# Decoder trunk: the opening reordered, small transfers postponed, modulation sums in every second projection step, their vectors to columns through DRAM

## The chip, the cores and the metric

The kernel runs on one core of one Trainium2 chip, in one launch. The metric is device time in microseconds (us); beside it a profile of one execution is read. TensorE (PE) multiplies matrices, VectorE (DVE), ScalarE (ACT) and GpSimd (POOL) work element by element, and SyncE (SP) issues most of the transfers (DMAs). Each engine runs its own list of instructions strictly in order, and waits on semaphores for the other engines and for DMAs.

## The reference, cut to what matters

Two layers, 512 rows of 1024 float32 each. A conditioning vector c gives six vectors of 1024 per layer (`mod`): shift, scale and gate for each half of the layer.

```python
cond = jax.nn.silu(c)
for l in range(DEPTH):                                   # 2
    mod = cond @ w_mod[l] + b_mod[l]                     # w_mod[l]: 1024 x 6144
    sh1, sc1, ga1, sh2, sc2, ga2 = [m[:, None, :] for m in jnp.split(mod, N_MOD, axis=-1)]

    h = rms_norm(x, g_norm1[l]) * (1.0 + sc1) + sh1
    z = h @ w_in[l]                                      # 1024 x 2560
    qa, ka, va, ub, qc, kc, vc = jnp.split(z, cuts, axis=-1)
    ...                                                  # heads, rms norm with gains, rope; three mixers ya, yb, yc
    y = jnp.concatenate([ya, yb, yc], axis=-1) @ w_out[l]
    x = x + ga1 * y

    h = rms_norm(x, g_norm2[l]) * (1.0 + sc2) + sh2
    x = x + ga2 * hier_moe(h, ...)                       # 32 experts, top 2 of one group
return x
```

## The kernel before

A layer is `front(l)` and then the experts (`moe`). The **opening** of `front` computes the first two of the six vectors (number i=0: shift and scale of the first half), normalizes x (`norm1`, ACT and DVE), transposes it on PE (L407), and splits each of its eight column blocks into a high and a low part (ACT L310, DVE or POOL L311), because a product of float32 is made of three passes (`mm3`, L314 to L316).

Then come the **projections**: five chunks of eight steps, step number 8c+j. A step is 12 matmuls of 128x512. Two steps share one megabyte of `w_in`, halves of which are split by ACT (L310) and POOL (L311) a little ahead (`split_next`). At a chunk's end the results go from PSUM to SBUF (`copy`, L320 on DVE and L322 on ACT, in turn). While chunk c runs, DVE, ACT and POOL normalize and rotate the heads of chunk c-1 (`rope_work`, L485 to L496, with tables that `tables` makes on POOL, L383 and L386), and PE transposes them (`heads_T`, L501). During the fifth chunk (UV) and after it run the mixers, PE's output projection, and the router.

**The modulation.** A product of the vector c with 1024 x 2048 of `w_mod` is read as eight pieces of 1 MB. For i=0 PE multiplies (`mod_unit`, L245). For i=1 (gate of the first half, shift of the second) and i=2 (scale and gate of the second) DVE adds up the pieces (`mod_part`, L253 and L255, 128x2048 each), one a step from step g on, PE adds over the partitions at step e (`mod_sum`, L260), and DVE adds the bias (`mod_row`, L270): the vectors then lie along one partition. `PLAN[l]` is (g, e) of i=1 and (g, e) of i=2. At step e + `LATER[l]` `mod_finish` brings a vector into columns, one number a partition, by 16 small matmuls with an identity (`to_cols`, L281) and a small DVE operation (L292, L297, L299), and spreads a gate over 128 partitions by way of DRAM (L288 writes `ga_d`, L289 reads it). The i=0 product of layer 1 is made by PE among the mixers of layer 0 (`one_mod`).

**Order.** PE, ACT, DVE and POOL are ordered by a scheduler; the PE and POOL work is also moved across the source's order. SP's queue is in the order of the program: all weights go through an arena of 1 MB buffers in the fixed order of `stream` (a planner sorts by the step at which each is needed, `want_layer`), and `pump` issues the next one as soon as a buffer is free. A DMA that has to wait on SP holds all that are behind it. The DMAs of SP and ACT use eight semaphores (DMAHW0 to 7) in turn, those of POOL eight others (DMASW); an instruction that uses one again waits for the DMA that had it before.

## Time and profile before

| | |
|---|---|
| median of 3 runs | 1226.66 us (1225.65 to 1226.69) |
| profiled execution, device time | 1228.5 us |
| its span | 1225.7 us |
| PE busy | 1072.6 us (88%) |
| DVE busy | 654.8 us (53%) |
| ACT busy | 358.2 us (29%) |
| POOL busy | 326.1 us (27%) |
| DMA, mean | 269 GB/s |

The span is that of the profiled execution from its first to its last instruction; the device time has 2.8 us more around it. Busy shares are means over stages with different limits: layer 0's front lies at about 0 to 285 us of the span, its experts from there to about 620, layer 1's front at about 620 to 880 and its experts behind. Views of stretches of the span tell more than the totals.

### The profile page before, as it was taken

The page shows a single profiled execution, that of the slowest core. Times are in us where ns is not written, and L with a number is a line of the kernel's source. Part 1 is how long each engine was busy: PE and PEld are TensorE (multiplying, and loading weights), DVE is VectorE, ACT ScalarE, POOL GpSimd, SP SyncE. Part 2 cuts the span into 40 slices and gives each one's busy share as a digit, 9 for nine tenths or more (in the row PEclk, how much of TensorE's full clock was granted, in tenths as well). Part 3 has the DMA queues.
Part 4 walks back from the last instruction along what each step waited for, and adds up shares of the span by engine and source line. Part 5 has one row for each costly group of instructions (what it writes and reads, how often), then busy time and mean ns, then how long its engine had stood idle before and what let it go on. Part 6 is the DMA issues. An engine that isn't in the chain of part 4 may idle for free. (4 is left out here: it accounts for less than half of the span.)

```text
span 1225.7 us, 14999 instructions
## 1 busy us (share of the span) xinstructions
PE 1072.6 (88%) x5134; PEld 627.1 (51%) x5134; DVE 654.8 (53%) x1333; ACT 358.2 (29%) x906; POOL 326.1 (27%) x259
## 2 busy tenths in 40 slices
PE   3878879999999988998877789999999999899784
PEld 2656757567783333333326567676778333333232
DVE  2779965657752222222269999767786222122127
ACT  2223223546441211111104233446643111111110
POOL 2585542000121211121116454520022312022010
PEclk9888988979989999999988898999999999999997
DMA  9946424752675999999995625352168899999993
GB/s 332 398 151 241 172 69 125 241 210 69 244 272 173 409 408 399 405 376 388 402 362 226 240 94 198 121 177 70 37 242 305 294 406 409 406 396 390 386 401 128
DMA packets 90476, 330.13 MB, mean 269 GB/s; under 512 B 18421, under 2 KB 22709, under 8 KB 75729
## 3 DMA queue, kind: packets, MB, share of 16 engines
q1 hardware_dynamic: 74248, 308.07, 66.0%
q0 software_dynamic: 15056, 18.01, 4.9%
q10 hardware_dynamic: 1016, 2.18, 0.5%
q8 instruction: 73, 1.20, 0.4%
q14 instruction: 83, 0.67, 0.2%
HBM read 339.10 MB, written 30.95 MB: 302 GB/s over the span
## 5 line engine op out<-in xcount | busy, mean ns | idle before, releaser
L1091 PE MATMUL ps<-unit,unit 128*64 128x512 f32 x1120 | 269.5, 607 | 19.1 <-DMA unit<-w 18.8
L314 PE MATMUL ps<-unit,unit 128*128 128x512 f32 x448 | 190.7, 432 | 16.4 <-DVE unit L320 16.0
L315 PE MATMUL ps<-unit,unit 128*128 128x512 f32 x448 | 185.3, 414 | 9.6 <-POOL unit L311 8.4
L1091 PEld LDWEIGHTS ps<-unit,unit 128*64 128x64 f32 x1120 | 88.7, 140 | 188.3 <-issue 171.6
L316 PE MATMUL ps<-unit,unit 128*128 128x512 f32 x448 | 183.0, 412 | 0.5 <-DVE unit L311 0.5
L1111 PE MATMUL ps<-unit,unit 128*64 128x512 f32 x560 | 140.0, 622 | 16.2 <-PEq L1159 14.5
L1096 DVE SCALAR_TENSOR_TENSOR unit<-ps,slot_f,unit 128x256 f32<-128x256 f32 x35 | 16.9, 484 | 248.7 <-ACT unit L1095 248.7
L311 POOL TENSOR_TENSOR unit<-unit,unit 128x1024 fp32r<-128x1024 f32 (+1 forms) x46 | 120.8, 2631 | 79.6 <-ACT unit L310 79.6
L1060 POOL DMA_INDIRECT unit<-xn_d,slot_i x62 | 63.1, 1018 | 288.6 <-PE ps L1071 158.0
L1095 ACT ACTIVATE unit<-ps 128x256 f32<-128x256 f32 x35 | 13.5, 385 | 392.5 <-PE ps L1091 392.5
L310 ACT ACTIVATE unit<-unit 128x1024 fp32r<-128x1024 f32 (+1 forms) x92 | 88.2, 964 | 133.1 <-PE ps L316 71.0
L314 PEld LDWEIGHTS ps<-unit,unit 128*128 128x128 f32 x448 | 90.2, 202 | 44.2 <-DVE unit L320 18.1
L315 PEld LDWEIGHTS ps<-unit,unit 128*128 128x128 f32 x448 | 90.4, 202 | 30.0 <-POOL unit L311 9.6
L316 PEld LDWEIGHTS ps<-unit,unit 128*128 128x128 f32 x448 | 89.4, 200 | 21.3 <-DVE unit L311 1.2
L1125 DVE TENSOR_TENSOR unit<-ps,unit 128x512 f32<-128x512 f32 x62 | 42.9, 692 | 84.6 <-PE ps L1111 84.6
L255 DVE SCALAR_TENSOR_TENSOR unit<-unit,csil,unit 128x2048 f32<-128x2048 f32 x28 | 85.0, 3034 | 0.4
L1111 PEld LDWEIGHTS ps<-unit,unit 128*64 128x64 f32 x560 | 36.1, 139 | 92.5 <-issue 60.5
L512 ACT ACTIVATE unit<-unit,sm 128x512 f32<-128x512 f32 (+3 forms) x96 | 53.3, 556 | 37.8 <-DVE sm L510 37.3
L1080 DVE TENSOR_SCALAR unit<-ps,cols 128x128 f32<-128x128 f32 x132 | 45.1, 404 | 33.5 <-PE ps L1071 33.5
L311 DVE TENSOR_TENSOR unit<-unit,unit 128x1024 fp32r<-128x1024 f32 (+1 forms) x46 | 56.6, 1236 | 9.4 <-ACT unit L310 8.7
L1065 POOL DMA_INDIRECT y_d<-unit,slot_y x31 | 31.5, 1016 | 111.3 <-DVEq L1161 46.5
L322 ACT ACTIVATE unit<-ps 128x512 f32<-128x512 f32 (+3 forms) x82 | 39.4, 487 | 73.1 <-PE ps L316 31.7
(215 smaller groups left out, 1409.7 us busy)
## 6 DMA issues: line engine op xcount, KB each, us to landing
unit<-w SPq DMA_DIRECT2D x256, 512.0 KB, 13.4
unit<-w SPq DMA_DIRECT2D x64, 1024.0 KB, 14.9
unit<-w_mod SPq DMA_DIRECT2D x48, 1024.0 KB, 4.7
unit<-w_in SPq DMA_DIRECT2D x16, 1024.0 KB, 14.2
y_d<-k_zero SPq DMA_DIRECT2D x16, 512.0 KB, 10.7
unit<-w_out SPq DMA_DIRECT2D x8, 1024.0 KB, 7.1
unit<-y_d SPq DMA_DIRECT2D x16, 512.0 KB, 12.0
unit<-w_in SPq DMA_DIRECT2D x8, 512.0 KB, 7.5
```

What stands on the lines that cost most here:

```text
L255: nc.vector.scalar_tensor_tensor(acc, w, csil[:, j:j + 1], acc, op0=OP.mult, op1=OP.add)
L310: nc.scalar.activation(hi.bitcast(F32R), src, AF.Copy)
L311: (eng or nc.gpsimd).tensor_tensor(lo.bitcast(F32R), src, hi, op=OP.subtract)
L314: nc.tensor.matmul(o, ahi.bitcast(F32R), bhi.bitcast(F32R), start=first, stop=False)
L315: nc.tensor.matmul(o, ahi.bitcast(F32R), blo.bitcast(F32R), start=False, stop=False)
L316: nc.tensor.matmul(o, alo.bitcast(F32R), bhi.bitcast(F32R), start=False, stop=last)
L512: nc.scalar.activation(dst[:, :n], dst[:, :n], AF.Exp, bias=mx, scale=-1.0, accum_out=z)
L1060: nc.gpsimd.indirect_dma_start(out=dst, out_offset=None, in_=xn_d, in_offset=bass.IndirectOffsetOnAxis(ap=idx, axis=0), bounds_check=S - 1 ...
L1080: nc.vector.tensor_scalar(dst[:, j, :], p, cols[:, SC2, j:j + 1], cols[:, SH2, j:j + 1], op0=OP.mult, op1=OP.add)
L1091: nc.tensor.matmul(ph[64 * r:64 * r + 64, :], xT[:, j, 64 * r:64 * r + 64], ws[:, j % 4], start=j == 0, stop=j == 7, tile_position=(0, 64 ...
L1111: nc.tensor.matmul(PS[banks[n]][64 * r:64 * r + 64, :], hidT[b][:, j, 64 * r:64 * r + 64], w2[r][:, j, n, :], start=j == 0, stop=j == 1, t ...
L1125: nc.vector.tensor_tensor(ys[b][:, cs], p, ga2[:, cs], op=OP.mult)
```

## The change

In words: `PLAN` gives other steps, and `mod_part` runs in every second step (g, g+2, ...) in place of eight in a row. `to_cols` goes, except for i=0 of layer 0 (`mod_cols0`); in its place `mod_spread`, right after `mod_row`, has SP write the four rows to DRAM (`mod_d`), read a vector back as 128x8 columns, and spread the gate from there. In layer 0's opening the gains and lambda (`gains`) come as rows of one partition on ACT's DMA queue and are spread by one PE matmul, the rope table comes on ACT's queue too, `tables` runs at POOL's start, `small_tables` goes behind the splits of the rows (`rows_in`), the scaling of `gsub` behind it, and PE's transposes are interleaved with `mod_unit`.

```diff
-PLAN = ((2, 15, 17, 30), (2, 14, 17, 30))
+PLAN = ((1, 18, 19, 35), (1, 18, 19, 35))
 LEAD = (3, 3)
-LATER = (3, 5)
+LATER = (4, 4)
 ROOM = (0, 2)
 EARLY = (0, 1, 2, 3, 4, 5, 6, 7)
-LATE = ((0, 3), (1, 6))
+LATE = (1, 6)
...
-        need += [(g + j, want_mod, (l, i, j, j + 1)) for i, g in ((1, g1), (2, g2)) for j in range(8)]
+        need += [(g + 2 * j, want_mod, (l, i, j, j + 1)) for i, g in ((1, g1), (2, g2)) for j in range(8)]
...
-    def mod_finish(l, i, bank):
-        def to_cols(c, *groups):
...
-        def bcast(dst, g):
...
+    def mod_cols0(bank):
...
+    def mod_spread(i):
+
+        row = mod_d[i:i + 1, :]
+        nc.sync.dma_start(row.rearrange("o (g n) -> (o g) n", g=4), mrow[0:128:32, :])
+        col = lambda h: row[:, D * h:D * h + D].rearrange("o (p j) -> (o p) j", j=8)
         if i == 0:
-            v = to_cols(0, 0, 2)
-            scaled(SC1, v[:, :, 1], G1)
-            nc.vector.tensor_copy(cols[:, SH1, :], v[:, :, 0])
+            nc.sync.dma_start(cols[:, SH1, :], col(0))
+            nc.sync.dma_start(cols[:, 6, :], col(1))
         elif i == 1:
-            nc.vector.tensor_copy(cols[:, SH2, :], to_cols(0, 2)[:, :, 0])
-            bcast(ga1_of[0], 0)
+            nc.sync.dma_start(cols[:, SH2, :], col(1))
+            nc.sync.dma_start(ga1_of[0], row[:, 0:D].to_broadcast([128, D]))
         else:
-            scaled(SC2, to_cols(0, 0)[:, :, 0], G2)
-            bcast(ga2, 2)
+            nc.sync.dma_start(cols[:, 6, :], col(0))
+            nc.sync.dma_start(ga2, row[:, D:2 * D].to_broadcast([128, D]))
+
+    def mod_finish(i):
+        if i == 0:
+            scaled(SC1, cols[:, 6, :], G1)
+        if i == 2:
+            scaled(SC2, cols[:, 6, :], G2)
...
+        def gains(q):
...
+            row = W[10][0:1, 0:512]
+            for n, g in enumerate(("gk_a", "gq_a", "gq_c", "gk_c")):
+                q.dma_start(row[:, HD * n:HD * n + HD], I[g][l:l + 1, :])
+            q.dma_start(row[:, 4 * HD:8 * HD], bass.AP(tensor=I["lam_a"].tensor, offset=I["lam_a"].offset + l * 4 * HD,
+                                                       ap=[[4 * HD, 1], [1, 4 * HD]]))
+            nc.tensor.matmul(PS[6], ones_f[0:1, 0:1].to_broadcast([1, 128]), row, start=True, stop=True)
+            nc.vector.tensor_copy(W[15], PS[6])
...
             tables()
-        if l == 0:
-            for j in range(8):
-                mod_unit(0, 0, j, 7)
-                pump(ROOM[l])
-            mod_row(7, W[14])
-            mod_finish(0, 0, 7)
-            nc.sync.dma_start(rope, I["k_rope"])
+            gsub_scaled()
+        else:
+
+            with tc.manual_schedule(engines={mybir.EngineType.PE, mybir.EngineType.Pool}):
+                gains(nc.scalar)
+                nc.scalar.dma_start(rope, I["k_rope"])
+                tables()
+                for m in range(NT):
+                    norm1(m)
+                for m in range(NT):
+                    for j in range(6):
+                        transposed(j, m)
+                    mod_unit(0, 0, m, 7)
+                    pump(ROOM[l])
+                for j in range(NT, 8):
+                    mod_unit(0, 0, j, 7)
+                    pump(ROOM[l])
+                mod_row(7, W[14])
+                for m in range(NT):
+                    transposed(6, m)
+                mod_cols0(7)
...
+        if l:
+            rows_in()
+        else:
+            with tc.manual_schedule(engines={mybir.EngineType.Pool}):
+                rows_in()
+                small_tables(nc.gpsimd)
+            gsub_scaled()
...
                         mod_row(7, W[11 + i])
+                        mod_spread(i)
                     if 8 * c + j == e + LATER[l]:
-                        mod_finish(l, i, 7)
-                    if 0 <= 8 * c + j - g < 8:
-                        mod_part(l, i, 8 * c + j - g, acc.ap)
+                        mod_finish(i)
+                    k, odd = divmod(8 * c + j - g, 2)
+                    if 0 <= k < 8 and not odd:
+                        mod_part(l, i, k, acc.ap)
                         pump(keep[0])
...
-                if l == 0 and (c, j) == LATE[0]:
-                    small_tables(nc.gpsimd)
-                    tables()
-                if l == 0 and (c, j) == LATE[1]:
+                if l == 0 and (c, j) == LATE:
                     masks(nc.sync)
...
                 mod_row(3, W[14])
-                mod_finish(ll, i, 3)
+                mod_spread(i)
+                mod_finish(i)
```

**The opening on SP.** The first transfers of SP's queue before (x, then seven of the eight pieces of `w_mod` for i=0; the waits are those on semaphores):

```order
L219 DMA unit_1_170<-x 128x2x1024
L219 DMA unit_2_171<-x 128x2x1024
L157 DMA unit_19_205<-w_mod 128x2048
L157 DMA unit_20_207<-w_mod 128x2048
L157 DMA unit_21_209<-w_mod 128x2048 [waits DMAHW0_49]
L157 DMA unit_22_211<-w_mod 128x2048 [waits DMAHW1_49]
L157 DMA unit_23_213<-w_mod 128x2048 [waits DMAHW2_49]
```

and the same of the changed kernel:

```order
L219 DMA unit_1_170<-x 128x2x1024
L219 DMA unit_2_171<-x 128x2x1024
L157 DMA unit_19_205<-w_mod 128x2048 [waits DMAHW4_49]
L157 DMA unit_20_207<-w_mod 128x2048 [waits DMAHW5_49]
L157 DMA unit_21_209<-w_mod 128x2048 [waits DMAHW6_49]
L157 DMA unit_22_211<-w_mod 128x2048 [waits DMAHW7_49]
L157 DMA unit_23_213<-w_mod 128x2048 [waits DMAHW0_49]
```

Before, the first two pieces went out without a wait; now the first waits for the DMA that had DMAHW4, which is `b_mod` on ACT's queue, and the second for the second half of x; the next three wait for rows of gains, which ACT's queue issues in between:

```order
L221 DMA ccol<-c 128x8
L222 DMA ident<-k_ident 128x128
L359 DMA cols<-g_norm 128x8
L265 DMA unit_11_197<-b_mod 4x512 [waits DVE_49]
L235 ACTIVATE sm<-ccol 128x8 [waits DMAHW1_49]
L374 DMA unit_10_196<-gk_a 1x64
L374 DMA unit_10_196<-gq_a 1x64
L374 DMA unit_10_196<-gq_c 1x64 [waits DMAHW0_49]
L374 DMA unit_10_196<-gk_c 1x64
L375 DMA unit_10_196<-lam_a 1x256 [waits DMAHW2_49]
L439 DMA unit_5_191<-k_rope 128x512 [waits DMAHW3_49]
```

In this queue, the third gain row waits for the first half of x, lambda for the identity and the rope table for `g_norm1`.

**Behind the splits of the rows, on POOL and DVE.** POOL before, from the splits of the rows (L311, 128x512) and of the weights (L311, 128x1024) to the tables and the next weights (three pairs of the twelve table rows are like the first):

```order
L311 TENSOR_TENSOR unit_12_198<-unit_28_282,unit_12_198 128x1024 [waits DMAHW7_49,Activation_49]
L311 TENSOR_TENSOR unit_18_204<-unit_9_195,unit_16_202 128x512 [waits Activation_49] x2
L311 TENSOR_TENSOR unit_13_199<-unit_28_282,unit_13_199 128x1024 [waits Activation_49]
L383 TENSOR_TENSOR unit_14_200<-unit_5_191,unit_11_197 128x256 [waits DMAHW5_49]
L386 TENSOR_TENSOR unit_14_200<-unit_5_191,unit_11_197 128x4x32 x2
```

and in the changed kernel:

```order
L313 TENSOR_TENSOR unit_12_198<-unit_28_299,unit_12_198 128x1024 [waits DMAHW5_49,Activation_49]
L313 TENSOR_TENSOR unit_18_204<-unit_9_195,unit_16_202 128x512 [waits Activation_49]
L381 DMA gsub<-g_sub_a 128x1
L382 DMA wpool<-w_pool 128x2x64
L383 DMA pcol<-b_pool 128x2x1
L384 DMA pcol<-pool_scale 128x2x1
L385 DMA cols<-g_norm 128x8
L265 DMA unit_11_197<-b_mod 4x512 [waits DMASW0_49]
L265 DMA unit_11_197<-b_mod 4x512 [waits DMASW1_49]
L313 TENSOR_TENSOR unit_13_199<-unit_28_299,unit_13_199 128x1024 [waits Activation_49]
```

The twelve operations of the tables are gone from here (they stand at POOL's start), and seven small transfers stand between the last split of a row and the weight split of buffer 13. DVE before, at the same place (last splits of the rows, sums of i=1, the first copies out of PSUM):

```order
L311 TENSOR_TENSOR unit_18_204<-unit_9_195,unit_16_202 128x512 [waits Activation_49]
L454 TENSOR_SCALAR unit_9_195<-ps_147,cols 128x512 [waits Pool_49]
L255 SCALAR_TENSOR_TENSOR unit_34_364<-unit_31_300,csil,unit_34_364 128x2048 [waits DMAHW2_49,DVE_49]
L255 SCALAR_TENSOR_TENSOR unit_34_364<-unit_32_306,csil,unit_34_364 128x2048 [waits DMAHW3_49,DVE_49]
L255 SCALAR_TENSOR_TENSOR unit_34_364<-unit_33_312,csil,unit_34_364 128x2048 [waits DMAHW4_49,DVE_49]
L255 SCALAR_TENSOR_TENSOR unit_34_364<-unit_35_367,csil,unit_34_364 128x2048 [waits DMAHW6_49,DVE_49]
L320 COPY unit_8_194<-ps_141 128x512 [waits PE_49]
```

and now:

```order
L253 TENSOR_SCALAR unit_34_404<-unit_29_311,csil 128x2048 [waits DMAHW6_49]
L313 TENSOR_TENSOR unit_18_204<-unit_9_195,unit_16_202 128x512 [waits Activation_49]
L411 TENSOR_SCALAR gsub<-gsub 128x1 [waits DMASW3_49]
L255 SCALAR_TENSOR_TENSOR unit_34_404<-unit_31_323,csil,unit_34_404 128x2048 [waits DMAHW0_49,DVE_49]
L255 SCALAR_TENSOR_TENSOR unit_34_404<-unit_32_329,csil,unit_34_404 128x2048 [waits DMAHW1_49,DVE_49]
L255 SCALAR_TENSOR_TENSOR unit_34_404<-unit_35_407,csil,unit_34_404 128x2048 [waits DMAHW3_49,DVE_49]
L322 COPY unit_8_194<-ps_141 128x512 [waits PE_49]
L322 COPY unit_8_194<-ps_143 128x512 [waits PE_49]
```

The scaling of `gsub` (L411) stands ahead of three sums and the two copies, and waits for its transfer from POOL's queue (DMASW3).

**The spread of i=1 on SP**, before:

```order
L232 DMA tok<-k_tok 128x8 [waits DMAHW4_49]
L288 DMA ga_d<-unit_3_172 2x512 [waits DMAHW5_49,DVE_49]
L289 DMA unit_4_190<-ga_d 128x1024 [waits DMAHW6_49,DMAHW5_49]
L157 DMA unit_48_794<-w_mod 128x2048 [waits DMAHW7_49,Pool_49]
L157 DMA unit_49_811<-w_mod 128x2048 [waits DMAHW0_49,DVE_49]
```

and now:

```order
L157 DMA unit_46_690<-w_in 128x4x512 [waits DMAHW1_49,DVE_49]
L289 DMA mod_d<-unit_3_172 4x512 [waits DMAHW2_49,DVE_49]
L295 DMA cols<-mod_d 128x8 [waits DMAHW3_49,DMAHW2_49]
L296 DMA unit_4_190<-mod_d 128x1024 [waits DMAHW4_49]
L157 DMA unit_48_818<-w_mod 128x2048 [waits DMAHW5_49,Pool_49]
L157 DMA unit_49_833<-w_mod 128x2048 [waits DMAHW6_49,DVE_49]
```

The read of the columns is added between the write, for which it waits, and the spreading of the gate. The first piece of `w_mod` behind belongs to step 23 now; before, it belonged to step 20.

## Rows read from the trace of the kernel before

Times are microseconds from the span's start, counts stand behind an x, and an arrow <- behind idle time names what ended it.

**Rows 1.** The page's head: busy time, share and instructions of each engine.

```profile
PE 1072.6 (88%) x5134; PEld 627.1 (51%) x5134; DVE 654.8 (53%) x1333; ACT 358.2 (29%) x906; POOL 326.1 (27%) x259
```

**Rows 2.** Stretches: PE, PEld, DVE, ACT, POOL busy, PE's clock, DMA share, GB/s.

```profile
180.00:200.00 20.00, 20.00 (x90) 13.36 (x90) 8.24 (x24) 7.41 (x16) 5.42 (x3) 0.83 0.24 79
790.00:810.00 20.00, 20.00 (x103) 14.58 (x102) 10.39 (x30) 8.94 (x21) 6.01 (x4) 0.91 0.24 84
```

**Rows 3.** Opening, stretches, same columns.

```profile
0.00:4.00 4.00, 0.00 (x0) 0.00 (x0) 1.72 (x6) 1.28 (x1) 2.94 (x9) 1.00 0.46 141
4.00:14.00 10.00, 0.00 (x0) 0.00 (x0) 1.18 (x7) 0.23 (x2) 4.86 (x9) 1.00 1.00 277
14.00:36.00 22.00, 13.30 (x92) 6.71 (x92) 5.40 (x8) 5.55 (x17) 0.28 (x1) 1.00 1.02 406
```

**Rows 4.** Opening, PE in order of time: start, length, instruction, idle before.

```profile
34.34 1.06 PE L245 MATMUL ps<-unit,csil 128*32 128x512 f32 x8 [1.43 <-DMA unit<-w_mod]
36.23 3.55 PE L281 MATMUL ps<-ident,unit 128*64 128x2 f32 x32 [0.81 <-DVE unit L270]
...
41.61 1.22 PE L314 MATMUL ps<-unit,unit 128*128 128x512 f32 x2 [0.39 <-ACT unit L310]
```

**Rows 5.** POOL's DMA queue in 0 to 16: packets, MB, share of 16 engines' time.

```profile
q0 software_dynamic: 342, 0.34, 22.0%
```

**Rows 6.** What PE waited for, 42 to 181 (layer 0's projections): total, times, longest.

```profile
PE ps L315 <- POOL unit L311: 8.4, 2, 6.2
PE ps L501 <- DVE unit L320: 6.1, 2, 3.6
PE ps L260 <- DVE unit L255: 6.0, 2, 4.8
PE ps L314 <- DVE unit L320: 3.1, 1, 3.1
```

**Rows 7.** Layer 0's projections, sum of the stretches from 40 to 180.

```profile
sum 140.00, PE 114.74 PEld 89.06 DVE 120.83 ACT 41.68 POOL 87.47; mean PE 16.39 PEld 12.72 DVE 17.26 ACT 5.95 POOL 12.50
```

**Rows 8.** POOL in order of time: an issue, last splits, first table, next splits.

```profile
40.27 0.58 POOL L750 DMA_DIRECT2D cols<-g_norm  x1 [2.59 <-DVE cols L297]
...
56.30 7.34 POOL L311 TENSOR_TENSOR unit<-unit,unit 128x512 fp32r<-128x512 f32 x2 [0.31 <-ACT unit L310]
63.61 2.77 POOL L383 TENSOR_TENSOR unit<-unit,unit 128x256 f32<-128x256 f32 x1
...
74.34 7.18 POOL L311 TENSOR_TENSOR unit<-unit,unit 128x1024 fp32r<-128x1024 f32 x2
```

**Rows 9.** DVE in order of time: four sums of i=1, first copy.

```profile
55.48 13.05 DVE L255 SCALAR_TENSOR_TENSOR unit<-unit,csil,unit 128x2048 f32<-128x2048 f32 x4
69.46 0.69 DVE L320 COPY unit<-ps 128x512 f32<-128x512 f32 x1 [0.93 <-PE ps L316]
```

**Rows 10.** DMAs issued in 36 to 41: KB each, us to landing.

```profile
cols<-g_norm POOLq DMA_DIRECT2D x1, 4.0 KB, 5.4
```

**Rows 11.** Costliest groups: instructions, busy and mean ns of one, idle before.

```profile
L255 DVE SCALAR_TENSOR_TENSOR unit<-unit,csil,unit 128x2048 f32<-128x2048 f32 x28 | 85.0, 3034 | 0.4
```

**Rows 12.** PE groups of the two small products, shapes apart.

```profile
L281 PE MATMUL ps<-ident,unit 128*64 128x1 f32 x128 | 14.2, 259 | 0.0
L260 PE MATMUL ps<-unit,ones_f 128*32 128x512 f32 x32 | 5.1, 719 | 6.0 <-DVE unit L255 6.0
```

**Rows 13.** Layer 1's projections, first stretch, and sum of those from 660 to 780.

```profile
660.00:680.00 20.00, 20.00 (x90) 16.76 (x89) 19.52 (x15) 7.67 (x11) 12.26 (x7) 0.97 0.62 214
...
sum 120.00, PE 104.45 PEld 82.67 DVE 113.06 ACT 38.56 POOL 63.77; mean PE 17.41 PEld 13.78 DVE 18.84 ACT 6.43 POOL 10.63
```

**Rows 14.** What PE waited for, 660 to 786.

```profile
PE ps L314 <- DVE unit L320: 12.9, 4, 7.8
```

**Rows 15.** What SP's queue waited for: the read of the gate.

```profile
SPq L289 <- DMA ga_d<-unit: 16.8, 4, 5.3
```

**Rows 16.** What PE waited for, 280 to 640: the weights of layer 0's experts.

```profile
PE ps L1091 <- DMA unit<-w: 6.6, 5, 2.1
```

More of the change, by code (lines that the diff above doesn't have):

```diff
@@ new lines, in mod_cols0 @@
+    def mod_cols0(bank):
+        v = mrow.rearrange("q (p j) -> q j p", j=8)
+        for j in range(8):
+            for r in range(2):
+                nc.tensor.matmul(PS[bank][64 * r:64 * r + 64, 2 * j:2 * j + 2], v[:, j, :],
+                                 ident[:, 32 * r:32 * r + 65:64], start=True, stop=True, tile_position=(0, 64 * r))
+        v = PS[bank][:, 0:16].rearrange("p (j n) -> p j n", n=2)
+        scaled(SC1, v[:, :, 1], G1)
+        nc.vector.tensor_copy(cols[:, SH1, :], v[:, :, 0])
@@ L394, in tables, with gsub_scaled, norm1, transposed @@
             nc.vector.tensor_scalar(lamt[:, 2:3], lamt[:, 2:3], -lam_init, None, op0=OP.add)
+        def gsub_scaled():
             nc.vector.tensor_scalar(gsub, gsub, 1.0 - lam_init, None, op0=OP.mult)
-        def norm1():
-            for m in range(NT):
-                nc.scalar.activation(W[4 + 2 * (m % 2)].bitcast(BF), X[m], AF.Square,
-                                     accum_out=sm[:, m:m + 1])
-                rstd_of(sm[:, 4 + m:5 + m], sm[:, m:m + 1], 1.0 / D)
-                nc.vector.tensor_scalar(xn[m], X[m].rearrange("p (q j) -> p j q", j=8),
-                                        sm[:, 4 + m:5 + m], None, op0=OP.mult)
-        def transposed(j):
-            for m in range(NT):
-                nc.tensor.transpose(PS[j][:, 128 * m:128 * m + 128], xn[m][:, j, :], ident)
+        def norm1(m):
+            nc.scalar.activation(W[4 + 2 * (m % 2)].bitcast(BF), X[m], AF.Square,
+                                 accum_out=sm[:, m:m + 1])
+            rstd_of(sm[:, 4 + m:5 + m], sm[:, m:m + 1], 1.0 / D)
+            nc.vector.tensor_scalar(xn[m], X[m].rearrange("p (q j) -> p j q", j=8),
+                                    sm[:, 4 + m:5 + m], None, op0=OP.mult)
+        def transposed(j, m):
+            nc.tensor.transpose(PS[j][:, 128 * m:128 * m + 128], xn[m][:, j, :], ident)
         if l:
+            gains(nc.gpsimd)
             small_tables(nc.gpsimd)
@@ L446, in split_next, with rows_in @@
                 pump(keep[0])
-        split_next()
-        transposed_last = False
-        for j in range(8):
-            if j == 7:
-                transposed(7)
-            t = W[4 + j % 4]
-            nc.vector.tensor_scalar(t, PS[j], cols[:, SC1, j:j + 1], cols[:, SH1, j:j + 1], op0=OP.mult, op1=OP.add)
-            split(hT[j], lT[j], t, nc.gpsimd if j % 2 else nc.vector)
+        def rows_in():
+            split_next()
+            for j in range(8):
+                if j == 7:
+                    for m in range(NT):
+                        transposed(7, m)
+                t = W[4 + j % 4]
+                nc.vector.tensor_scalar(t, PS[j], cols[:, SC1, j:j + 1], cols[:, SH1, j:j + 1], op0=OP.mult, op1=OP.add)
+                split(hT[j], lT[j], t, nc.gpsimd if j % 2 else nc.vector)
+        if l:
+            rows_in()
[4 more added lines that the diff above has]
+            gsub_scaled()
         for u in xnu:
```

38 lines of the change are left out of this document (14 added, 24 removed).

## The prediction, made before the changed kernel was run

> **What bounds the kernel now.** I start with the page's head: PE is busy 88% of the span, DVE 53% [rows 1]. That is a mean, so the views of stretches come next. From 180 to 280 us and again around 800, where the fifth chunk and the mixers run, PE is busy 20.00 of 20 us and DVE 8 to 13 [rows 2]: there each microsecond of PE work that goes is a microsecond of time. In the projections ahead of it the picture turns. Of the 140 us from 40 to 180 PE has 114.7 and DVE 120.8 [rows 7]; in layer 1, of 120 us, PE 104.5 and DVE 113.1 [rows 13]. PE at full rate issues 90 matmuls in 20 us [rows 13], so a step of 12 takes 2.67 us and the 32 steps that fill the 140 us would need 85. The rest is waits, and matmuls at the lower of PE's two clocks behind them. The view of waits says on whom: POOL's splits 8.4 us, DVE's copies 6.1 and 3.1, DVE's sums 6.0 [rows 6]; in layer 1 DVE's copies, 12.9 [rows 14]. So the projections are set by DVE's in-order list, with POOL once ahead of it. The opening is set by transfers: the DMA engines are full from 4 us on, yet move only 277 GB/s from 4 to 14 against 406 behind [rows 3], and PE's last `mod_unit`, at 34.34, has waited 1.43 us for its piece [rows 4]. In the experts PE waited 6.6 us for weights [rows 16], and these are loaded as buffers come free, so I take a gain ahead of them as moving the whole rest of the chain: it counts once, in full.
>
> All sums are against the span of the profiled run, 1225.7 us; its device time, 1228.5, lies 1.8 above the median, 1226.66. I subtract the gain from the median.
>
> **1. The opening.** Software-queue transfers took 22.0% of 16 engines in 16 us, that is 3.5 us, for 0.34 MB [rows 5]. The gains, the bulk of them (32 KB four times and 128 KB), become rows of one partition, and `small_tables` goes away from here. Against that, the rope table comes in ahead, 0.26 MB or 0.65 us at 406 GB/s, and the first piece of `w_mod` waits until `b_mod` has landed, while before it queued right behind x. What must land by 34.3 is x and eight pieces, 10.5 MB, and 0.4 MB of others: at 406 GB/s 27 us. With a start at about 2.6 us (141 GB/s over the first four are 1.4 us' worth at 406) [rows 3], nothing lost would give 29.4, a gain of 5. The wait leaves the engines without `w_mod` from the end of x and `b_mod` until the first piece flows, which I bound by 0 and 5 us, the whole of what is freed, and put at 2.5. **Gain 2.5 (0 to 5).** The added matmul and copy of the gains and the tables on POOL lie under the same transfers: POOL is busy 0.28 of 22 us from 14 to 36 [rows 3]; were that cover gone, 10.7 us of tables would show. The rest of the chain, `mod_row`, 16 matmuls in 3.55 us, two column operations, to the first projection at 41.61 [rows 4], is the same in both.
>
> **2. Layer 0, steps 0 to 31.** The tables go from POOL's list, where they lay from 63.61 to 74.34 ahead of weight splits that PE wanted, 10.7 us [rows 8]; the larger part of the 8.4 us wait [rows 6], with the slow clock behind it, is theirs. In their place stand seven DMA issues; at 0.58 us for each [rows 8] that is 4.1 us, less than half. But DVE now waits for the first of them. DVE came to its four sums at 55.48 [rows 9], so to `gsub` at about 53.5 when all is 2.5 earlier. On POOL the last row split and the weight split behind it took 7.34 us to 63.6 [rows 8], so the row split ended near 60; the issue stands between the two now, at about 57.5, and a small POOL transfer took 5.4 us to land [rows 10]. DVE waits till about 63: 9 us. Behind it are three sums, at 3.26 us each as in the row of four [rows 9] 10 us, and the two copies, without which PE doesn't get the next chunk's PSUM: they come at 73, against the 69.46 of before [rows 9]. PE would have been held until 77 there by POOL, so the new wait replaces most of the old one and leaves some 3 us of gain. What comes behind is DVE's sum: 120.8 us of work in the stretch [rows 7], less one sum that goes past step 31 (3.03 us [rows 11]) and a few tenths of column operations: 117. Idle of before was 19 us; I put 9 for `gsub` and 5 for all others: 131 against 140. The halved rate of sums is what lets the copies and rotations come through in time; if it does nothing, the other idle time is 16, and the stretch 142; if all of it goes, 126. **Gain 9 (-2 to 14).**
>
> The Trainium skill, in "DMA: Bandwidth & Descriptors", section "Anatomy of one DMA — SWDGE (gpsimd) path", gives a fixed cost of about 2.0 us for a DMA of this kind. The row above has 5.4 [rows 10], taken under full DMA engines. By the page `gsub` would land 3.4 us sooner and the total would come out at about 1200; the measured one is used.
>
> **3. What PE loses in stretches that it fills.** The 16 matmuls of `to_cols` cost 3.55 us each time [rows 4]; 192 records in two shapes are six times [rows 12]. One stays. Of the five that go, that of i=1 lies where DVE sets the pace in either layer, and three lie in PE's own stretches [rows 2]: i=2 of either layer at steps 33 and 35 in the fifth chunk, and i=0 of layer 1 among the mixers. That is 10.7 us. Into the fifth chunk comes the `mod_sum` of i=2 (step 35 for 30) in both layers: four matmuls of 0.72 us at the mean [rows 12], overlapped to about 1.1 a time, 2.2 in all. **Gain 8.5 (5 to 10.7).** The columns now come by SP: a write, a wait of 4.2 us in the mean and 5.3 at most (16.8 in 4) [rows 15], then a read of 128 pieces of 32 B, like `g_norm`'s, which landed in 5.4 [rows 10]. That is about 10 us against `LATER`, four steps or 10.7: just in time. If not, DVE stands for a microsecond in a chunk where it has 7 of 20 us free [rows 2].
>
> **4. Layer 1's projections.** The opening there is not changed. DVE is at 113 of 120 us [rows 13]; one sum of 3.03 goes past step 31, and the waits for copies, 12.9 [rows 14], can shrink only as far as DVE's 7 us of idle allow. **Gain 3 (-5 to 7)**: the lower end is one round trip of 5.3 that PE waits for in full.
>
> Sum: 2.5 + 9 + 8.5 + 3 = 23. 1226.7 - 23 = **1203.7 us**. All ends together would be 1190 and 1229.
>
> **Rivals.**
> *A. DVE stays as late as it was.* The wait for `gsub` takes all that the tables gave, and layer 1 gains nothing: 2.5 + 8.5 = 11, so 1215.7. For it: 9 us on an engine with 19 idle. Against: these 19 are mostly waits for POOL and PE that the tables caused. Chance 0.2.
> *B. PE becomes the bound in the projections.* With waits gone the matmuls run at the upper clock too, and each part comes out at its upper end: 1190. Against: DVE's work alone is 117 us in a stretch where PE needs 85. Chance 0.1.
> *C. Slower: SP's round trips.* Every `mod_spread` holds all weight loads behind it on SP. Were each of the five (layer 0 has i=1 and i=2, layer 1 all three) to cost PE a write, 5.3, and a read, 5.4, in full, 54 us would go; the kernel is slower from 23 us on, that is with three of the five: 1203.7 + 32 = 1236. Against: the same queue had such a wait four times already [rows 15], and the piece behind the first belongs to step 23, five steps or 13.4 us behind the write. Chance 0.08.
> The Trainium skill's "DMA: Bandwidth & Descriptors", section "Specifications", wants pieces of 512 B at least for the full rate; the columns' are 32 B. That speaks for C, but at 4 KB the row of 5.4 us [rows 10] already holds such pieces.
> *D. No change.* The experts' weights arrive at their own pace and PE waits there for what the fronts won: 1226. For it: PE does wait for weights there. Against: 6.6 us in 360 [rows 16], and loads that start when PE frees a buffer. Chance 0.07.
> The forecast has the remaining 0.55.
>
> The range, 1193 to 1219, holds the forecast's own spread, A, and part of B. Some 0.2% or 2.5 us is what a measurement of this kernel tells from no change; faster by more 0.85, within it 0.06, slower by more 0.09.
>
> **What would show it.** In the changed profile: the last `mod_unit` at about 32; no POOL wait of 6 us near 71, and an idle DVE of 6 to 10 us ahead of L411; the copies behind it a few microseconds after PE asks; step 32 near 170; L281 with 32 records only, and the fifth chunk and mixers shorter by 2.5 and 3.5 us; layer 1's projections within 5 us of before; the experts as long as before. I would be wrong if DVE is idle for much more than 9 us, if PE waits for `w_mod` in steps 19 to 33, or if the experts become longer by what the fronts gained.

## The result

The changed kernel takes 1193.08 us (median of 4 runs, 1191.14 to 1194.48); the kernel before, beside it, 1226.68. The ratio is 0.9724, with an interval of 0.9705 to 0.9743. The change is faster by 33.6 us where 23 were forecast; by the ratio the time stands at 1192.8, a little below the range's lower end of 1193.0. A second set of runs on another chip gave 1194.92 us and 0.973 (0.9703 to 0.9757); in its trace every step of the projections starts within 1.4 us of where it starts in the first.

The page of the changed kernel, in the columns of [rows 1]:

```profile
PE 1044.9 (88%) x4976; PEld 601.3 (50%) x4976; DVE 651.3 (55%) x1331; ACT 356.8 (30%) x906; POOL 316.7 (27%) x254
```

PE is busy 27.7 us less, though it has only 158 matmul records fewer: the 160 of five `to_cols`, which took 17.8 us (five times 3.55), are gone, and the two of the matmul that spreads the gains have come. Where the rest came from is the question of this document. I cut both traces at the same instructions: the first matmul of the first projection step (step 0), of steps 32 and 39, the start of the last product of the output projection, and the end of PE's last matmul, which lies 6.4 us (before) and 6.6 us (changed) ahead of the span's end. Lengths in us:

```
stretch                                   before    after   change  forecast
start to step 0, layer 0                   41.61    38.84     -2.8     -2.5
steps 0 to 31, layer 0                    139.56   130.06     -9.5     -9
steps 32 to 38, layer 0                    39.19    34.29     -4.9     -2.5
step 39, mixers, output projection, l. 0  117.58   108.66     -8.9     -3.5
experts, layer 0, to step 0 of layer 1    322.81   321.95     -0.9      0
steps 0 to 31, layer 1                    124.64   122.18     -2.5     -3
steps 32 to 38, layer 1                    38.16    34.29     -3.9     -2.5
step 39, mixers, output projection, l. 1  101.03   101.01      0.0      0
experts, layer 1                          294.70   294.77     +0.1      0
```

Terms 1, 2 and 4 came out within about 0.5 us. The excess is in the third, in the stretches that PE fills (steps 32 to 38 of both layers, and layer 0's mixers): 17.7 us for 8.5. There the granted clock differs. Windows of the kernel before, PE's clock in the third column from the end; the small matmuls ran from 184.1 to 187.7 and from 259.8 to 263.3:

```profile
184.00:188.00 4.00, 4.00 (x35) 3.86 (x36) 0.92 (x2) 0.00 (x0) 0.00 (x0) 0.83 0.76 261
188.00:192.00 4.00, 4.00 (x10) 2.01 (x9) 1.31 (x4) 1.52 (x4) 0.61 (x1) 0.50 0.42 136
...
262.00:266.00 4.00, 4.00 (x22) 3.11 (x22) 2.20 (x11) 0.87 (x3) 0.00 (x0) 0.50 0.28 113
266.00:270.00 4.00, 4.00 (x13) 2.61 (x12) 0.73 (x4) 0.52 (x3) 0.00 (x0) 0.50 0.00 0
270.00:274.00 4.00, 4.00 (x12) 2.92 (x13) 1.89 (x10) 2.41 (x11) 0.00 (x0) 0.50 0.00 0
```

The same places in the changed kernel:

```profile
172.00:176.00 4.00, 4.00 (x17) 2.45 (x18) 3.93 (x8) 0.54 (x1) 0.00 (x0) 1.00 0.85 299
176.00:180.00 4.00, 4.00 (x16) 2.56 (x16) 2.39 (x9) 3.06 (x8) 1.99 (x1) 1.00 0.54 225
...
248.00:252.00 4.00, 4.00 (x24) 3.16 (x24) 3.15 (x12) 2.87 (x11) 0.00 (x0) 1.00 0.01 1
```

PE is busy 4.00 of 4 in all of them, with or without the small matmuls; what tells them apart is the clock, 0.50 (1.2 GHz) against 1.00 (2.4 GHz). The busy column alone, which I read before, hides it. Longer windows around each of the three runs of small matmuls (the third, in layer 1, from 796.4 to 799.9) give the price of the clock:

```profile
184.00:196.00 12.00, 12.00 (x56) 8.28 (x56) 3.85 (x10) 2.58 (x5) 0.95 (x2) 0.72 0.39 132
258.00:278.00 20.00, 20.00 (x101) 14.94 (x98) 8.87 (x36) 7.57 (x30) 0.00 (x0) 0.66 0.25 87
798.00:806.00 8.00, 8.00 (x41) 5.85 (x42) 2.62 (x8) 2.12 (x5) 0.00 (x0) 0.79 0.00 0
```

A stretch of 12 us at a mean clock of 0.72 lacks 0.28 of 12, 3.4 us of full clock; the other two lack 6.8 and 1.7. With the matmuls' own 3.55 us that makes 6.9, 10.4 and 5.2 us, an estimate that takes all of PE's work there as bound by the clock.

The opening went as forecast. PE in order of time, as in [rows 4]: the last `mod_unit`, transposes, the 16 small matmuls that stay, and the first projection step:

```profile
31.99 1.94 PE L245 MATMUL ps<-unit,csil 128*32 128x512 f32 x8 [0.56 <-DMA unit<-w_mod]
33.86 1.12 PE L421 MATMUL ps<-ident,unit 128*128 128x128 f32 x4
34.91 2.09 PE L280 MATMUL ps<-ident,unit 128*64 128x2 f32 x32
...
38.84 0.80 PE L316 MATMUL ps<-unit,unit 128*128 128x512 f32 x1 [0.39 <-ACT unit L312]
```

Layer 0's projections in the changed kernel (38 to 169), what PE waited for, as in [rows 6]:

```profile
PE ps L540 <- DVE unit L322: 14.8, 3, 5.4
PE ps L316 <- DVE unit L322: 3.7, 2, 2.5
PE ps L317 <- POOL unit L313: 3.3, 3, 1.9
```

POOL's 8.4 us are down to 3.3, and the waits for sums (L260) are gone; but the transposes of the heads (L540, L501 of before) wait 14.8 for VectorE's copies where it was 6.1. DVE's own list shows the wait that I had put at 9 us:

```profile
58.53 0.15 DVE L411 TENSOR_SCALAR gsub<-gsub 128x1 f32<-128x1 f32 x1 [6.51 <-DMA gsub<-g_sub_a]
58.63 10.28 DVE L255 SCALAR_TENSOR_TENSOR unit<-unit,csil,unit 128x2048 f32<-128x2048 f32 x3
68.83 1.28 DVE L322 COPY unit<-ps 128x512 f32<-128x512 f32 x2
```

It is 6.51, because POOL reached the issue at 53.12 and not at 57.5; the sums behind it took the 10 us of the forecast, and the copies came at 68.8 for 73.

### The profile page after: what moved, and what is told of

The parts are those of the page before. It is cut to its first block, busy times and chain, and to the rows that moved or that the text cites. A ratio compares the mean times of both kernels' runs of the same rounds, so it can differ in the third digit from the quotient of the medians.

```text
span 1192.7 us, 14678 instructions
## 1 busy us (share of the span) xinstructions
PE 1044.9 (88%) x4976; PEld 601.3 (50%) x4976; DVE 651.3 (55%) x1331; ACT 356.8 (30%) x906; POOL 316.7 (27%) x254
## 5 line engine op out<-in xcount | busy, mean ns | idle before, releaser
L316 PE MATMUL ps<-unit,unit 128*128 128x512 f32 x448 | 185.9, 421 | 9.0 <-DVE unit L322 8.3
L317 PE MATMUL ps<-unit,unit 128*128 128x512 f32 x448 | 181.9, 406 | 7.8 <-POOL unit L313 6.5
L318 PE MATMUL ps<-unit,unit 128*128 128x512 f32 x448 | 179.6, 404 | 0.5 <-DVE unit L313 0.5
L1150 PE MATMUL ps<-unit,unit 128*64 128x512 f32 x560 | 135.9, 604 | 10.1 <-PEq L1198 8.5
L316 PEld LDWEIGHTS ps<-unit,unit 128*128 128x128 f32 x448 | 87.5, 196 | 36.2 <-DVE unit L322 10.0
L317 PEld LDWEIGHTS ps<-unit,unit 128*128 128x128 f32 x448 | 87.5, 196 | 28.3 <-POOL unit L313 8.6
L318 PEld LDWEIGHTS ps<-unit,unit 128*128 128x128 f32 x448 | 86.9, 195 | 20.1 <-DVE unit L313 1.2
L255 DVE SCALAR_TENSOR_TENSOR unit<-unit,csil,unit 128x2048 f32<-128x2048 f32 x28 | 80.3, 2868 | 3.6 <-DMA unit<-w_mod 3.4
L1150 PEld LDWEIGHTS ps<-unit,unit 128*64 128x64 f32 x560 | 35.8, 136 | 83.6 <-issue 74.3
L1119 DVE TENSOR_SCALAR unit<-ps,cols 128x128 f32<-128x128 f32 x132 | 45.1, 405 | 33.6 <-PE ps L1110 33.6
L313 DVE TENSOR_TENSOR unit<-unit,unit 128x1024 fp32r<-128x1024 f32 (+1 forms) x46 | 53.1, 1160 | 9.2 <-ACT unit L312 8.7
```

The source lines that it names most:

```text
L255: nc.vector.scalar_tensor_tensor(acc, w, csil[:, j:j + 1], acc, op0=OP.mult, op1=OP.add)
L313: (eng or nc.gpsimd).tensor_tensor(lo.bitcast(F32R), src, hi, op=OP.subtract)
L316: nc.tensor.matmul(o, ahi.bitcast(F32R), bhi.bitcast(F32R), start=first, stop=False)
L317: nc.tensor.matmul(o, ahi.bitcast(F32R), blo.bitcast(F32R), start=False, stop=False)
L318: nc.tensor.matmul(o, alo.bitcast(F32R), bhi.bitcast(F32R), start=False, stop=last)
L1119: nc.vector.tensor_scalar(dst[:, j, :], p, cols[:, SC2, j:j + 1], cols[:, SH2, j:j + 1], op0=OP.mult, op1=OP.add)
```

## The experiments

Two theories for the excess. **Clock**: the small matmuls cost their own 3.55 us and, behind them, matmuls at 1.2 GHz. **Time only**: they cost their 3.55 us, and the rest comes from elsewhere. Times are medians; "by the trace" compares the stretches of the table with the changed kernel's (for the spread alone, with those of the kernel before). The sets ran on several chips, on which the kernel before took 1225.0 to 1228.1 us, so a difference of a few us between two sets is read from the stretches.

**Columns on PE again** (the rest of the change kept; at step 37 the small matmuls lie over eight columns of a head's output in PSUM, so that part of the result is not the reference's).

```diff
-LATER = (4, 4)
+LATER = (2, 2)
...
-            nc.sync.dma_start(cols[:, SH2, :], col(1))
...
+            nc.vector.tensor_copy(cols[:, SH2, :], to_cols(bank, 2)[:, :, 0])
```

> The changed kernel with the columns made by 16 small matmuls on PE again at i=1, i=2 and layer 1's i=0 (two steps behind the sum, in place of the read back from DRAM). Theory 'clock': the small matmuls cost their 3.55 us and leave PE at the lower of its two clocks for some microseconds behind, as before showed behind 184 and 260 us (granted clock 0.50 from 188 to 192 and from 262 to 274). Then the three in stretches that PE fills cost what the two traces differ by there: about 6 in layer 0's fifth chunk, 9 in its mixers and output projection, 5 in layer 1's fifth chunk, 20 us in all, so 1213 or a little more from the two of i=1. Theory 'time only': each costs its own 3.55 us where PE is busy without a break, 10.7 us for three, so 1204, and the rest of the unexpected gain lies elsewhere.

1221.47 us, ratio to before 0.9965 (0.9947 to 0.9983). By the trace 6.4 us in layer 0's fifth chunk, 6.1 from there to the end of its output projection, 5.1 in layer 1's fifth chunk: 17.6 us for three, and 7 in the projections. "Time only" (10.7) is out. The total, 28 us above the change, is more than either gave: 20 for the three, and the two of i=1 in the projections cost more than the little that "clock" left for them.

**The spread alone**, put into the kernel before (its old plan, opening and tables).

```diff
                         mod_row(7, W[11 + i])
+                        mod_spread(i)
...
-                        mod_finish(l, i, 7)
+                        mod_finish(i)
```

> The kernel before with one part of the change alone: mod_spread in place of the 16 small matmuls for i=1, i=2 and layer 1's i=0 (at the old steps, sums every step, old opening). Theory 'clock': the three in stretches that PE fills give about 6, 9 and 5 us, and those of i=1 little: -17 to -22 us against before. Theory 'time only': -10.7, at most -17 if those of i=1 count too. Theory 'round trips': the longer chains on SP hold the weights, and less than 5 is won.

1210.25 us, 0.9864 (0.9844 to 0.9885): -16.4. By this total "clock" (-17 to -22) is just missed, and "time only" could stand with its -17; the stretches decide. By the trace 6.2, 8.9 and 5.2 us go in the three that PE fills, 20.3 in all, where "time only" has 10.7; steps 0 to 31 are the same in layer 0 and 3.9 longer in layer 1, so those of i=1 gave nothing. (The opening's 16 small matmuls have the changed kernel's order here too; the stretch up to step 0 is 0.3 us shorter.) The clock is 1.00 in all three places:

```profile
184.00:196.00 12.00, 12.00 (x51) 7.77 (x52) 6.96 (x22) 6.22 (x14) 3.02 (x2) 1.00 0.25 88
250.00:270.00 20.00, 20.00 (x127) 14.20 (x126) 15.24 (x60) 12.31 (x43) 0.00 (x0) 1.00 0.34 116
766.00:774.00 8.00, 8.00 (x37) 5.78 (x36) 3.19 (x8) 4.01 (x8) 2.59 (x2) 1.00 0.20 69
```

So the excess belongs to this part of the change, and "round trips" is out: in the changed kernel SP issued the read of i=1 at 121.70, 1.8 us after the write at 119.90, and its five reads waited 8.1 us for their writes, 3.4 at most.

**Small and full matmuls at step 33.** Sixteen small ones, and sixteen of 128x512, added to the changed kernel in both layers.

```diff
+                        nc.tensor.matmul(PS[7][64 * r:64 * r + 64, k:k + 1], v[:, k, :], ident[:, 0:1],
+                                         start=True, stop=True, tile_position=(0, 64 * r))
...
+                    nc.tensor.matmul(PS[7], hT[k % 8][:, 0:128].bitcast(F32R), hT[k % 8].bitcast(F32R),
+                                     start=True, stop=True)
```

> The changed kernel with 16 more small matmuls (a column of the identity each, their result is not used) at step 33 of either layer, where PE is busy without a break. Theory 'clock': 3.55 us and the lower clock behind, 5 to 6 us a layer, so +10 to +12 (1203 to 1205), and the granted clock falls to 0.5 in the four microseconds behind. Theory 'time only': +7.1 (1200), and the clock stays at 1.00.

> The same place, but 16 matmuls of 128x512 like those of a projection step (result not used), which take 16 times 0.227 us, 3.6 us, at the upper clock. Both theories: +7.3 us for the two layers (1200) and no fall of the clock. If this costs as much as the small ones, the clock has nothing to do with it.

Small: 1211.75 us, 0.9884 (0.9839 to 0.9928). Full: 1198.52, 0.977 (0.9736 to 0.9805). By the trace the full ones cost 3.4 us in either layer, the small ones 3.3 in layer 0 and 4.9 in layer 1. The small ones ran from 174.7 to 178.3 and from 772.4 to 776.0; the windows at their end and behind them, layer 0 and layer 1:

```profile
176.00:180.00 4.00, 4.00 (x31) 3.69 (x32) 2.95 (x8) 1.52 (x4) 0.00 (x0) 1.00 0.99 397
180.00:184.00 4.00, 4.00 (x18) 2.47 (x17) 1.36 (x5) 2.00 (x4) 1.55 (x1) 1.00 0.06 23
...
776.00:780.00 4.00, 4.00 (x12) 2.82 (x12) 1.14 (x3) 0.48 (x2) 0.00 (x0) 0.66 0.53 205
```

The clock fell in one layer and not in the other, with the same matmuls at the same step; where it did not fall, they cost about their own time. With the full ones it is 1.00 in both. So "clock" holds in one layer of two, and there at 4.9 us, a little under its price; by the total (1211.75) neither theory has it. Of this kernel's loss of 18.7 us by the trace only 8.1 lies in these two places; 5.7 lies in layer 0's experts (last section), 3.5 in the projections and 1.3 in layer 1's experts.

**The same pair in layer 0's mixers**, where before lost the most.

```diff
                 mod_spread(i)
+                        nc.tensor.matmul(PS[3][64 * r:64 * r + 64, 2 * k:2 * k + 2], v[:, k, :],
+                                         ident[:, 32 * r:32 * r + 65:64], start=True, stop=True,
+                                         tile_position=(0, 64 * r))
...
+                    nc.tensor.matmul(PS[3], ident, mrow, start=True, stop=True)
```

> The changed kernel with the 16 small matmuls of layer 1's i=0 back in layer 0's mixers (their result is not used; the columns still come from DRAM). Theory 'clock': 3.55 us and the lower clock behind them, as before had from 262 to 274, so layer 0's front ends 6 to 9 us later and the granted clock is 0.5 in the eight microseconds behind. Theory 'what follows': the clock fell before through what stood behind them, layer 0's front ends 3.6 us later and the clock stays at 1.00.

> At the same place four float32 products of 128x512 (the identity with the row of vectors, result not used), 16 passes of the array and so about 3.6 us at the upper clock. Both theories: layer 0's front ends 3.6 to 4.2 us later, and the clock stays at 1.00; a fall here would mean that any 3.6 us put in at this place brings it.

Small: 1207.08 us, 0.9843 (0.9817 to 0.9868). Full: 1199.53, 0.9784 (0.975 to 0.9819). By the trace, from step 39 to the end of the output projection the small ones cost 4.4 us, the full ones 2.7, though they ran 3.7 us on PE. (The rest of the small ones' 13 us lies in layer 0's experts, 3.6, and in the projections, 1.2 and 3.4.) The window behind the small ones, and the same one with the full ones:

```profile
248.00:252.00 4.00, 4.00 (x18) 2.92 (x17) 1.76 (x9) 1.89 (x8) 0.00 (x0) 0.60 0.06 12
```

```profile
248.00:252.00 4.00, 4.00 (x28) 2.68 (x27) 1.46 (x9) 1.77 (x8) 0.00 (x0) 1.00 0.08 21
```

So the small ones do bring the clock down there, and full ones of their length don't: "what follows" is out. But the fall is shorter than before's, which held 0.50 from 262 to 274, and its price is smaller than 6 to 9. What it is about the small ones (one or two columns moving, a load of weights for each, 64 of 128 columns in use) no run here takes apart.

**The plan of the sums.** One kernel has the pieces in eight steps in a row, with the partition sums where the change has them; the other has the whole old plan.

```diff
-PLAN = ((1, 18, 19, 35), (1, 18, 19, 35))
+PLAN = ((2, 18, 19, 35), (2, 18, 19, 35))
...
-PLAN = ((1, 18, 19, 35), (1, 18, 19, 35))
+PLAN = ((2, 15, 17, 30), (2, 14, 17, 30))
```

> The changed kernel with the pieces of the sums due in eight steps in a row (from steps 2 and 19), everything else, the steps of mod_sum too, as in the change. Theory 'spacing': the halved rate is what lets copies and rotations through, and without it the projections lose what they won: +5 to +12 (1198 to 1205). Theory 'order': DVE does the same work between the same copies, and the scheduler places the sums among the same neighbours: within 3 us of 1193.

> The changed kernel with the old plan of the sums (one a step from steps 2 and 17 or 14, partition sums at steps 15 and 30), all else as in the change. Theory 'spacing': as with the sums in a row from 2 and 19 (+20 us), the copies come late behind rows of sums, and +8 to +15 is lost (1201 to 1208). Theory 'collision': that run lost because its second row of sums came late, at 19 to 26, together with the late partition sum; the old plan has it earlier and costs within 4 us of the change.

In a row: 1213.37 us, 0.9904 (0.9868 to 0.994). Old plan: 1206.2, 0.9833 (0.9799 to 0.9867). "Spacing" holds in both, in the first beyond what it gave. With the old plan, and the tables out of POOL's way, steps 0 to 31 of layer 0 take 139.5 us by the trace, as before (139.6); those of layer 1 take 128.4, 6.2 more than in the change. In either layer 1.3 us of the difference is the `mod_sum` of i=2, which the old plan has at step 30 and the change behind step 31.

**The tables behind the row splits again**, the halved plan kept.

```diff
-                tables()
...
                 small_tables(nc.gpsimd)
+                tables()
```

> The changed kernel with the twelve table operations on POOL behind the row splits and the seven issues again, ahead of the weight splits, the rest of the change kept. Theory 'tables': PE waits there for POOL's weight splits some 6 us as before, and what the rows of before showed of it (8.4 us and the lower clock behind) comes back: +5 to +10 at step 10. Theory 'DVE sets the pace': the stall at step 7 lies under that for VectorE's copies, and the projections end within 3 us of the change's.

1207.41 us, 0.9839 (0.98 to 0.9877). Steps 0 to 31 take 140.5 us. What PE waited for in them:

```profile
PE ps L317 <- POOL unit L313: 18.7, 5, 14.7
PE ps L540 <- DVE unit L322: 12.2, 3, 5.3
```

Against the changed kernel's 3.3 for POOL this is one wait of 14.7 us, more than twice the 6 that was expected, and at step 10 the loss is 12.8 us. "Tables" holds, beyond its price. The two runs together: either part undone gives back the 9.5 us, so neither brought anything there without the other. A reserve: the tables stand here behind the seven issues too, 4.5 us on POOL (53.12 to 57.58 in the changed kernel) that before had elsewhere, so this run does not show the halved plan with before's POOL list as it was.

**gsub's transfer first**, so that DVE does not wait for it.

```diff
+                nc.gpsimd.dma_start(gsub, I["g_sub_a"][l].rearrange("(p o) -> p o", o=1))
                 gains(nc.scalar)
```

> The changed kernel with the transfer of gsub back at the head of POOL's queue, so that VectorE does not wait for it behind the row splits (6.5 us of idle ahead of L411 in the changed kernel's trace). Theory 'DVE sets the pace': the three sums and two copies behind come 6.5 us earlier, PE's wait of 2.45 us at the start of the second chunk goes, and 2 to 6 us are won (1187 to 1191). Theory 'slack': the next wait for VectorE, 5.4 us near 93 us, is set by what comes later, and takes it all: within 2 us.

1190.4 us, 0.9703 (0.9682 to 0.9724); the change on the same chip 1194.92. By the trace steps 0 to 31 are 2.8 us shorter, the opening is 1.3 longer (DVE now stands 4.9 us for `gsub` there), and 2.5 come in layer 0's experts. PE's waits for copies at the start of a chunk go from 3.7 us to 0.6, as "DVE sets the pace" has it, and its waits ahead of the transposes stay (14.8 and 15.0), so "slack" is out. But of DVE's 6.5 us PE had felt only these 3.1.

**Even steps.**

```diff
-PLAN = ((1, 18, 19, 35), (1, 18, 19, 35))
+PLAN = ((0, 16, 18, 34), (0, 16, 18, 34))
```

> The changed kernel with the sums on even steps (from 0 and 18, partition sums at 16 and 34), so that none falls on the last step of a chunk, where VectorE has copies to make. Theory 'copies': PE's waits for VectorE's copies, 14.8 us in layer 0 and 11.8 for the transposes in layer 1, shrink by a third or more: -4 to -12. Theory 'order': VectorE's list has the same sums between the same copies, because the scheduler sets the places: within 4 us of the change.

1198.93 us, 0.976 (0.9731 to 0.9789): a loss of 4 to 6 us against the two sets of the change. "Copies" is out: the waits of L540 are 16.2 us in layer 0 and 11.4 in layer 1. "Order" (within 4) is just missed too. By the trace 1.5 us go in layer 0's projections, 3.2 in layer 1's, and 2.2 in layer 0's steps 32 to 38, where PE waits 1.4 us for a softmax of DVE.

**Copies on ScalarE.** The 14.8 us of L540 are three waits, for copies that stand in DVE's list behind a sum (two) or a rotation (one). ACT is idle two thirds of the time there. First the copies of the heads, then those of the chunks too.

```diff
-                copy(m + k, d[:, :, 128 * m:128 * m + 128],
+                copy(0, d[:, :, 128 * m:128 * m + 128],
...
-            z_chunk(lambda m: copy(m, z[m], PS[m]), each)
+            z_chunk(lambda m: copy(0, z[m], PS[m]), each)
```

> The kernel with gsub's transfer first, and the copies of the transposed heads out of PSUM all on ScalarE (before, every second on VectorE behind its sums). Theory 'queue': PE's transposes waited 15.0 us in layer 0 and some 11 in layer 1 only because these copies stood behind sums on VectorE: -10 to -20 against the kernel with gsub first (1170 to 1180). Theory 'DVE sets the pace': the transposes then wait for the rotation that makes their input, also VectorE's, and 0 to 4 us are won.

> The same, and the copies of the first four chunks' results on ScalarE too. Theory 'queue': PE's waits for VectorE's copies at the start of a chunk (0.6 us in layer 0 with gsub first, 4.6 in layer 1) go as well: 2 to 6 us better than with the heads' copies alone. Theory 'ACT': four copies of 0.49 us behind one another hold the next chunk's first matmuls longer than two on either engine, and it is 0 to 4 us slower than that.

Heads: 1182.7 us, 0.9622 (0.9591 to 0.9653), the best of all. All: 1185.34, 0.9659 (0.9627 to 0.969). With the heads' copies on ACT the waits of L540 for copies are gone in layer 0, and PE waits elsewhere:

```profile
PE ps L316 <- DVE unit L322: 6.9, 1, 6.9
PE ps L317 <- POOL unit L313: 4.9, 5, 1.9
PE ps L542 <- DVE unit L537: 2.5, 1, 2.5
```

15.0 us of one wait go, and 6.3 come in another (0.6 before): DVE is later at the start of a chunk. Against the kernel with gsub first the median is 7.7 us lower, between the two theories; by the trace the projections alone are 5.4 and 5.2 us shorter in the two layers, the lower price of "queue", and the two expert stages 1.3 and 2.4 longer. So "queue" holds for the waits, at its lower price. With all copies on ACT, PE waits 12.0 us for POOL's splits in layer 0, and yet the projections are another 3.5 and 3.0 us shorter, as "queue" has it. What loses is the stretch behind them, 4.7 and 6.0 us in steps 32 to 38: PE stands 3.0 us for a softmax of DVE (L562) in either layer, where the other kernel has no wait, and works at a clock of 0.61 in layer 0's window behind and 0.50 in layer 1's.

```profile
PE ps L562 <- DVE sm L551: 3.0, 1, 3.0
```

```profile
165.70:169.70 4.00, 4.00 (x12) 2.98 (x11) 2.95 (x8) 1.52 (x4) 0.00 (x0) 0.61 0.42 176
...
747.60:751.60 4.00, 4.00 (x10) 2.66 (x9) 2.92 (x9) 1.52 (x4) 0.00 (x0) 0.50 0.50 207
```

"ACT" is right in the total, 2.6 us slower, but the loss does not lie where it had put it: at the start of the chunks PE waits for ACT only 1.9 us in layer 0 and 3.0 in layer 1, and these are waits for splits. Why the softmax comes late is not shown.

## Why the prediction was off

**The opening** was right: 2.8 for 2.5, the last `mod_unit` at 31.99 for 32, and the first piece of `w_mod` did go out only at 9.09, behind `b_mod`. One sentence was not: the rest of the chain is not "the same in both". The 16 small matmuls took 2.09 us there for 3.55 [rows 4]. `mod_cols0` gives them in another order, the two halves of the output's partitions in turn, where `to_cols` does one half and then the other; every kernel here with this order has 2.1. Eight transposes that now stand around them take up what this gives.

**Layer 0's steps 0 to 31** came out at 9.5 for 9, but not as I told it, and the agreement is luck in its parts. I gave the tables some 3 us at step 8 and the rest to fewer waits. At step 8 the gain is 2.5, at step 10 it is 7.9, at step 24 it is 1.2 and at step 32 again 9.5; and in the runs above neither the tables nor the halved plan brings anything without the other. DVE's work came to 112.9 us where I had 117, and its idle time to 17.1 where I had 14 (39 to 169): two errors that offset each other. The sentence that held is that the new wait for `gsub` replaces part of the old one: 6.5 us for 9. For its landing I weighed a row of 5.4 against the 2.0 of the Trainium skill ("DMA: Bandwidth & Descriptors", section "Anatomy of one DMA — SWDGE (gpsimd) path"): issued at 53.12, it released DVE at 58.53, 5.4 us later. The measurement decides, and the page's figure is too low for this place.

**What PE loses in stretches that it fills** is the step that failed: "That is 10.7 us", three times 3.55, with 10.7 as the upper bound. The three are worth 20.3 us in the kernel that has this part alone: 6.2, 8.9 and 5.2. The table agrees: 17.7, and 2.7 for the `mod_sum` that came into the fifth chunks (steps 32 to 38 take 34.29 us with it and 32.96 without, in either layer; I had put 2.2). The mechanism, that PE's time counts in full there, was right; the size left out that the matmuls behind small ones run at 1.2 GHz, which I put at nothing without a reason. The estimate from the clock above, 6.9, 10.4 and 5.2, 22.5 in all, lies a little above what was measured. The clock of 0.83 stood in [rows 2], beside the 20.00 of 20 that I quoted, and the view that it was taken from has 0.66 from 260 to 280. (It was misread in a second place, on which little rests: DVE is busy 7.8 to 14.9 us of 20 there, not 8 to 13.) Shown is that the excess goes with the small matmuls (alone, and undone), that the clock behind them is low where they cost more than their time, and that full matmuls of the same length don't bring it down. Not settled is when it falls and for how long: sixteen small matmuls cost 6.2, 8.9 and 5.2 us in the kernel before, but 3.3 and 4.9 at step 33 and 4.4 in the mixers when added to the changed one; the lower clock held for more than 12 us in the first mixers and some 3 in the second, and at one step 33 the clock did not fall. The Trainium skill ("TensorE: Matmul & The Clock Gate", section "HAM oscillation — how this bites in real kernels") tells of such falls for an engine that waits for transfers; here the windows show PE busy 4.00 of 4 and no wait, so the trace goes beyond the page.

**Layer 1's projections** were right in size, 2.5 for 3, but not in kind. I had the waits for VectorE's copies shrink. They were 12.9 us ahead of the projections' matmuls [rows 14] and 2.6 ahead of the transposes, and are 16.4 now (below: the changed kernel, 633 to 756). The 2.5 is a difference of two parts that I did not see: with the spread alone the stretch is 3.9 us longer than before, and the halved plan is worth 6.2 there, 1.3 of it the `mod_sum` that left. Why the spread costs 3.9 with the old plan stays open: PE waits 9.8 us ahead of the transposes in that kernel, for copies, and DVE waits for no transfer there.

```profile
PE ps L540 <- DVE unit L322: 11.8, 3, 4.9
PE ps L316 <- DVE unit L322: 4.6, 2, 3.1
```

**The rivals.** A did not come, though its wait did. B's time was nearly reached, but not B: PE still waits 22.7 us in layer 0's projections. C was wrong: SP's reads waited 1.6 us for their writes in the mean, where I had put 4.2 and 5.3 at most, and DVE waited for a piece of `w_mod` 1.7 us, once in layer 0's projections. D was wrong: the experts took as long as before.

## What to carry to other kernels

Where PE is busy all the time, read its clock beside its busy time, in windows behind each run of small matmuls: the price of these is their own time and what follows at the lower clock, here 3.3 to 8.9 us for 3.55 of their own. Before a stall is priced at its full length, look for what stands at the same place on the other engines, since either half of a pair of causes can be worth nothing without the other. And where an in-order engine sets the pace, a short copy behind a long operation is the first thing to give to an engine that is idle: that was worth 7.7 us here, while giving it the other copies too brought nothing in the total. And the same small matmuls took 2.09 us in one order and 3.55 in another, which is worth trying before they are moved off PE; no run here tried it in the stretches that PE fills.

## What was not expected

The experts of layer 0 are the same code in all kernels, but took 318.0 to 327.7 us by the traces. Part of it is PE's sequencer at the branches ahead of the second matmul of an expert (L1111, L1150 and so on). In the kernel before, 280 to 640, and in the changed one, 311 to 634:

```profile
PE ps L1111 <- PEq L1159: 10.3, 14, 3.4
```

```profile
PE ps L1150 <- PEq L1198: 4.1, 14, 0.3
...
PE ps L1130 <- DMA unit<-w: 11.4, 8, 2.3
```

Over the whole span it is 14.5 to 19.8 us in before and in three of the kernels with added matmuls on PE, and in the one with the columns on PE again; 12.1 in the one with full matmuls at step 33; and 8.0 to 8.5 in the changed kernel and all those with its 4976 PE instructions (and in the spread alone, 4974). It may be a matter of where the code lies; no run here shows it. Between before and the change it cancels: PE waits 6.2 us less for its sequencer and 4.8 more for weights. In the kernel with small matmuls at step 33 it does not cancel: PE waits 10.8 us for its sequencer in layer 0's experts, where the changed kernel has 4.1. So its loss of 18.7 us is not the price of the matmuls alone.
